# The last two gate blocks of a decoder layer, computed by halves of the tokens

## The chip, the cores and the metric

The kernel runs on one core of a Trainium2 chip. The metric is the time of the whole program on the device, in microseconds. The time before is 2029.54 us, the median of three runs (2029.25 to 2031.34).

## The reference

One decoder layer over 256 positions with 2048 features, in float32: a half-step SwiGLU, a mixer of a gated linear recurrence and a short convolution, a second half-step SwiGLU, then the part that the change touches:

```
gate = sigmoid(rms_norm(h, norm_ple) @ w_ple_gate)      # 2048 x 2048
h = h + gate * (p @ w_ple)                              # p has 256 features
return rms_norm(h, norm_final)

def rms_norm(x, g):
    r = rsqrt(mean(x * x, axis=-1) + EPS)               # over the features
    return x * r * g
```

The last norm needs the squares of all 2048 features of a token before it can scale any of them. Tokens are independent of each other in this stage.

## The kernel before, in words

Everything is kept transposed: `hT` is 128 partitions x 16 feature blocks x 256 tokens. A weight matrix is cut into blocks of 128 output features; a block is one *step* of a list. For a step, SP loads the block's weights (16 tiles of 128x128, 1 MB), two calls (L97 on ACT, L98 on DVE) split them into a high and a low part of type fp32r, and PE multiplies. The moving operand `xs[:, k, :]` holds for each of the 16 feature tiles the high part of 256 tokens and then their low part, 512 columns. `product` (L116) issues two matmuls per tile: the high weights with all 512 columns, and the low weights with the 256 high columns; both add up in one PSUM tile of 128x512, whose halves are added at the end (L146, L147). `product_one` (L124) issues three matmuls of 256 columns into the same 256 columns of PSUM, so that nothing is left to be added after the last one; it is used for the last block of a stage, where the next stage waits.

The stage at the end is `ple` (L787). Its 16 steps are the 16 blocks of `w_ple_gate`. The epilogue of a block (L824) multiplies by the row scale `rb` of the norm before (L153) and takes the sigmoid (L828). One step later `gated` (L850) multiplies by the block of p @ w_ple, adds to `hT`, adds the square to the running sum `acc` (L182, L183), and writes `hg`, the new h times the gain of the last norm (L855). The products p @ w_ple (L814) are spread over the earlier steps.

Block 15, the last, has an epilogue of its own: gate, sum and square by halves of the tokens in turn (L832 to L841), and a matmul with the squares as weights and one column of ones (L196) sums over the features, giving one number per token, on the token's partition; the running sum `acc` is added in the same way before it. After the loop over the steps (L958 to L969) the mean and the reciprocal root are made on 128x2 numbers (L201, then ten DVE instructions in `rsqrt`, L169), the result is put on the diagonal of two 128x128 tiles (L963), and a matmul with ones (L965, plain fp32, which PE executes as two passes) spreads it over all partitions. DVE multiplies `hg` by it in six pieces of 1, 2, 3, 3, 3 and 4 blocks (L968), and SP writes each piece out (L969).

The order of the work: the program is written step by step, and a planner orders the instructions of each engine by the time at which it expects their inputs. Between equally ready instructions the one written first goes first. On the chip each engine takes its queue in order and waits on semaphores. PSUM has eight buffers of 128x512 in rotation, the high and low parts of weights four of half a block each, small temporaries six.

Of the kernel before, what the change touches and what calls it, by code (L numbers as in the profile page):

```python
# [7 lines left out]
F32 = mybir.dt.float32  # L8
F32R = mybir.dt.float32r
I32 = mybir.dt.int32  # L10
AF = mybir.ActivationFunctionType
ALU = mybir.AluOpType
PSUM = bass.MemoryType.PSUM

P = 128
T = 256
T2 = 2 * T
NB = 16
NF = 44
NH = 8  # L20
EPS = 1e-6
# [6 lines left out]
C_FFN1, C_MIX, C_FFN2, C_PLE, C_FIN = 0, 16, 32, 48, 64  # L28
# [23 lines left out]
def kernel(  # L52
# [3 lines left out]
    nc = tc.nc  # L56
    V, A, TE = nc.vector, nc.scalar, nc.tensor
# [7 lines left out]
    hT = const.tile([P, NB, T], F32, name="hT")  # L65
    xs = const.tile([P, NB, T2], F32R, name="xs")
    cst = const.tile([P, NCST], F32, name="cst")
    ones = const.tile([P, P], F32, name="ones")
    ones_r = const.tile([P, P], F32R, name="ones_r")
    sel = const.tile([P, 2 * P], F32R, name="sel")  # L70
    acc = const.tile([P, T], F32, name="acc")
    rb = const.tile([P, T], F32, name="rb")
    rt = const.tile([P, 2], F32, name="rt")
# [3 lines left out]
    ident = cst[:, C_ID:C_ID + P]  # L77

    def tt(shape=(P, T), dtype=F32, tag="t", bufs=6):
        return tmp.tile(list(shape), dtype, tag=tag, name=tag, bufs=bufs)  # L80
# [49 lines left out]
    def weights(s, k):  # L130
        hi, lo = s.parts[k // s.half]
        return hi[:, k % s.half, :], lo[:, k % s.half, :]

    def products(s, ps, rhs, start=True, stop=True, ks=None, one=False):
        ks = range(s.nk) if ks is None else ks
        f = product_one if one else product
        for i, k in enumerate(ks):
            f(*weights(s, k), rhs(k), ps, start and i == 0, stop and i == len(ks) - 1)

    def new_ps():  # L140
        return psum.tile([P, T2], F32, tag="ps", name="ps")


    def halves(ps):
        t = tt()
        A.activation(t, ps[:, T:], AF.Copy)  # L146
        V.tensor_tensor(t, ps[:, :T], t, ALU.add)  # L147
        return t

    def scaled(ps, dst=None):  # L150
        t = halves(ps)
        dst = t if dst is None else dst
        V.tensor_tensor(dst, t, rb, ALU.mult)  # L153
        return dst
# [6 lines left out]
    def two(dst, src):  # L161
        A.activation(dst[:, :T], src, AF.Copy)  # L162
        V.tensor_tensor(dst[:, T:], src, dst[:, :T].bitcast(F32), ALU.subtract)
# [5 lines left out]
    def rsqrt(dst, v):  # L169
        V.tensor_scalar(dst.bitcast(I32), v.bitcast(I32), -0.5, MAGIC, ALU.mult, ALU.add)  # L170
        for _ in range(3):
            t = tt(shape=dst.shape)
            V.scalar_tensor_tensor(t, v, -0.5, dst, ALU.mult, ALU.mult)
            V.tensor_tensor(t, t, dst, ALU.mult)
            V.scalar_tensor_tensor(dst, t, 1.5, dst, ALU.add, ALU.mult)
# [19 lines left out]
    def token_sum(ps, src, i, first, last):  # L195
        TE.matmul(ps[i][:, 0:1], src[:, i * P:(i + 1) * P], ones[:, 0:1], start=first, stop=last)  # L196

    def token_scale(ps):
        v = tt(shape=(P, 2), tag="v2", bufs=1)
        for i in range(2):  # L200
            V.tensor_scalar(v[:, i:i + 1], ps[i][:, 0:1], 1.0 / (NB * P), EPS, ALU.mult, ALU.add)  # L201
        rsqrt(rt, v)
# [18 lines left out]
    steps = []  # L221

    def at(i, f):
        steps[i].hooks.append(f)

    def add(*a, **k):
        steps.append(Step(*a, **k))
        return len(steps) - 1

    st = {}  # L230

    def gemm_in(epi, one=False):
        def mm(s):
            s.ps = new_ps()
            products(s, s.ps, lambda k: xs[:, k, :], one=one)
        return mm, (lambda s: epi(s.ps))
# [549 lines left out]
    def ple():  # L786
        i0 = len(steps)  # L787
        m = st["ple"] = {}

        def open_ple(s):  # L790
            st["pool"] = ExitStack()
            p1 = m["pool"] = st["pool"].enter_context(tc.tile_pool(name="ple1", bufs=1))
            m["p"] = p1.tile([P, 2, T], F32, name="p")
            m["px"] = p1.tile([P, 2, T2], F32R, name="px")
            m["w"] = p1.tile([P, NB, 2 * P], F32, name="wpe")
            m["pe"] = p1.tile([P, NB, T], F32, name="pe")
            m["hg"] = p1.tile([P, NB, T], F32, name="hg")
            nc.sync.dma_start(m["p"], pT)
            for j in (0, 8):
                nc.sync.dma_start(m["w"][:, j:j + 8, :], w_pe[:, j:j + 8, :])  # L800

        def p_parts():
            for k in range(2):
                two(m["px"][:, k, :], m["p"][:, k, :])

        def pe_parts(j):
            hi = m["pool"].tile([P, 2, 2 * P], F32R, tag="pwh", name="pwh", bufs=2)
            lo = m["pool"].tile([P, 2, 2 * P], F32R, tag="pwl", name="pwl", bufs=2)
            w = m["w"][:, j:j + 2, :]
            A.activation(hi, w, AF.Copy)  # L810
            V.tensor_tensor(lo, w, hi.bitcast(F32), ALU.subtract)
            st["pw", j] = hi, lo

        def pe_mm(j):  # L814
            hi, lo = st["pw", j - j % 2]
            ps = new_ps()
            for k in range(2):
                sl = slice(k * P, (k + 1) * P)
                product(hi[:, j % 2, sl], lo[:, j % 2, sl], m["px"][:, k, :], ps, k == 0, k == 1)
            t = tt()  # L820
            A.activation(t, ps[:, T:], AF.Copy)
            V.tensor_tensor(m["pe"][:, j, :], ps[:, :T], t, ALU.add)

        def gate_epi(j):  # L824
            def epi(ps):
                s = st["s", j] = m["pool"].tile([P, T], F32, tag="sg", name="sg", bufs=4)
                if j < NB - 1:
                    A.activation(s, scaled(ps), AF.Sigmoid)  # L828
                    return
                token_sums_first()  # L830
                z, sq, h, pe = tt(), tt(), hT[:, j, :], m["pe"][:, j, :]
                for i in range(2):  # L832
                    a = slice(i * P, (i + 1) * P)
                    V.tensor_tensor(z[:, a], ps[:, a], rb[:, a], ALU.mult)
                    A.activation(s[:, a], z[:, a], AF.Sigmoid)
                for i in range(2):
                    a = slice(i * P, (i + 1) * P)
                    V.tensor_tensor(s[:, a], s[:, a], pe[:, a], ALU.mult)
                    V.tensor_tensor(h[:, a], h[:, a], s[:, a], ALU.add)
                    A.activation(sq[:, a], h[:, a], AF.Square)  # L840
                    token_sum(st["ts"], sq, i, False, True)  # L841
                A.activation(m["hg"][:, j, :], h, AF.Copy, scale=cst[:, C_FIN + j:C_FIN + j + 1])
            return epi

        def token_sums_first():
            st["ts"] = new_ps(), new_ps()
            for i in range(2):
                token_sum(st["ts"], acc, i, True, False)

        def gated(j):  # L850
            s, h = st["s", j], hT[:, j, :]
            V.tensor_tensor(s, s, m["pe"][:, j, :], ALU.mult)
            V.tensor_tensor(h, h, s, ALU.add)
            square_sum(j)
            A.activation(m["hg"][:, j, :], h, AF.Copy, scale=cst[:, C_FIN + j:C_FIN + j + 1])  # L855

        for j in range(NB):
            add(w_pg[j], NB, *gemm_in(gate_epi(j), one=j == NB - 1))
        at(i0, p_parts)
        for j in range(0, NB, 2):  # L860
            at(i0 + 1 + j // 2, lambda j=j: pe_parts(j))
            for d in range(2):
                at(i0 + 2 + j // 2, lambda j=j + d: pe_mm(j))
        for j in range(NB - 1):
            at(i0 + max(j, 2 + j // 2), lambda j=j: gated(j))
        steps[i0].before = open_ple
        return i0
# [30 lines left out]
    with tc.manual_schedule():  # L898
        for a, b in pieces:
            s = steps[a // 8]  # L900
# [10 lines left out]
        for j in range(NB):  # L911
            sq = sums[j] if j < 2 else tt()
# [41 lines left out]
        if s.after:  # L954
            s.after(s)


    m = st["ple"]  # L958
    ps = st["ts"]
    token_scale(ps)  # L960
    dg = tt()
    for i in range(2):
        V.tensor_scalar(dg[:, i * P:(i + 1) * P], ident, rt[:, i:i + 1], None, ALU.mult)  # L963
    ps = new_ps()
    TE.matmul(ps[:, :T], ones, dg, start=True, stop=True)  # L965
    for a, b in ((0, 1), (1, 3), (3, 6), (6, 9), (9, 12), (12, 16)):
        o = m["hg"][:, a:b, :]
        V.tensor_tensor(o, o, ps[:, :T].unsqueeze(1).broadcast_to([P, b - a, T]), ALU.mult)  # L968
        nc.sync.dma_start(out[:, a:b, :], o)  # L969
    st["pool"].close()  # L970


# [68 lines left out]
```

## Time and profile before

| | us |
|---|---|
| median of three runs | 2029.54 |
| the profiled execution | 2028.77 |
| its span | 2027.0 |
| PE busy in the span | 2002.1 |
| DVE busy | 1636.0 |
| ACT busy | 1117.1 |

The profile is of one execution. Its time is the span and 1.77 us around it. PE is the matmuls, PEld the loads of weights into PE, DVE and ACT the vector and scalar engines, SP the engine that issues the DMAs. A row such as `L196 PE MATMUL ps<-ones,acc 128*128 128x1 f32 x4` gives the line, engine and operation, the output and inputs by name, the shape, and how many instructions the row stands for. Matmuls are pipelined, so their listed durations overlap; the distance from start to start is what one costs. PEclk is the granted clock of PE as a share of 2.4 GHz.

### The profile page before, as it was taken

What the parts mean: (1) busy time and instruction counts of PE and PEld (TensorE: products, weight loads), DVE (VectorE), ACT (ScalarE), POOL (GpSimd) and SP (SyncE); (2) the same over time, 40 slices, a digit from 0 to 9 for tenths busy, and PEclk for the clock granted to TensorE, in tenths of its full rate; (3) what the DMA queues carried; (4) which work ended last, traced back from release to release, by engine and by line L of the source; (5) the groups of instructions that cost most, each with busy time, mean ns of one, the idle gap of its engine ahead of it and who ended that gap; (6) DMA issues with size and microseconds to landing.
All of it is one profiled execution on the core that took longest, in us unless ns stands there. A gap on an engine that the chain in (4) does not pass through costs nothing.

```text
span 2027.0 us, 28859 instructions
## 1 busy us (share of the span) xinstructions
PE 2002.1 (99%) x11094; PEld 1731.7 (85%) x11094; DVE 1636.0 (81%) x2645; ACT 1117.1 (55%) x1716; POOL 11.6 (1%) x23
## 2 busy tenths in 40 slices
PE   8999999999999999999999999999999999999997
PEld 7888888888888888888888888888888888888886
DVE  8988886888688775689798789788968886887886
ACT  7655555555555554553566556455555555555663
POOL 0000000000000000000000000000000000000000
PEclk9999999999999999999999999999999999999998
DMA  8686666665665465544355567766666666654742
GB/s 293 211 277 242 233 205 216 219 237 200 222 232 198 156 212 187 189 166 146 129 184 187 187 227 274 226 232 226 208 208 224 232 202 220 228 202 153 249 164 84
DMA packets 69546, 419.93 MB, mean 207 GB/s; under 512 B 7712, under 2 KB 7968, under 8 KB 35744
## 3 DMA queue, kind: packets, MB, share of 16 engines
q1 hardware_dynamic: 67104, 407.60, 59.0%
q0 software_dynamic: 2304, 10.49, 1.3%
q8 instruction: 87, 1.43, 0.3%
q14 instruction: 51, 0.42, 0.1%
HBM read 405.48 MB, written 12.58 MB: 206 GB/s over the span
## 4 chain that ended last, share of the span: by engine, by line
PE 89%; DVE 4%; DMA 4%; issue 1%; ACT 1%; SPq 0%; DVEq 0%; ACTq 0%
PE ps L120 49%; PE ps L119 23%; PE ps L294 3%; PE ps L295 3%; PE ps L293 3%; PE ps L122 2%; DVE lo L98 2%; DMA sraw<-w1s 1%; DMA raw<-w1d 1%; DMA raw<-w1u 1%; PE ps L591 1%; PE ps L494 1%; PE ps L493 1%; PE ps L492 1%; DMA sraw<-w2s 1%
## 5 line engine op out<-in xcount | busy, mean ns | idle before, releaser
L120 PE MATMUL ps<-xs,hi 128*128 128x512 f32 x3056 | 1082.8, 395 | 9.5 <-DVE xs L167 6.1
L98 DVE TENSOR_TENSOR lo<-raw,hi 128x1024 fp32r<-128x1024 f32 (+2 forms) x660 | 751.1, 1139 | 239.3 <-ACT hi L97 235.7
L97 ACT ACTIVATE hi<-raw 128x1024 fp32r<-128x1024 f32 (+2 forms) x660 | 652.7, 990 | 516.6 <-PE ps L120 323.6
L119 PE MATMUL ps<-xs,lo 128*128 128x256 f32 x2865 | 801.5, 280 | 0.4 <-DVE lo L98 0.2
L120 PEld LDWEIGHTS ps<-xs,hi 128*128 128x128 f32 x3056 | 569.7, 188 | 137.5 <-ACT hi L97 7.2
L119 PEld LDWEIGHTS ps<-xs,lo 128*128 128x128 f32 x2865 | 538.0, 188 | 10.4 <-DVE lo L98 1.8
L120 PE MATMUL ps<-hid,hi 128*128 128x512 f32 x1384 | 477.6, 394 | 0.0
L119 PE MATMUL ps<-hid,lo 128*128 128x256 f32 x1258 | 354.4, 283 | 0.5 <-ACT hid L162 0.5
L120 PEld LDWEIGHTS ps<-hid,hi 128*128 128x128 f32 x1384 | 251.5, 188 | 48.8
L119 PEld LDWEIGHTS ps<-hid,lo 128*128 128x128 f32 x1258 | 236.2, 188 | 7.3 <-ACT hid L162 1.3
L309 ACT ACTIVATE ahi<-sraw 128x1024 fp32r<-128x1024 f32 x48 | 51.0, 1063 | 125.2 <-DMA sraw<-w1s 61.5
L146 ACT ACTIVATE t<-ps 128x256 f32<-128x256 f32 x191 | 70.2, 372 | 88.3 <-PE ps L120 88.3
L320 DVE TENSOR_TENSOR st<-sraw 128x1024 f32<-128x1024 f32 x48 | 58.8, 1224 | 69.2 <-DMA sraw<-w1s 38.7
L147 DVE TENSOR_TENSOR t<-ps,t 128x256 f32<-128x256 f32 x191 | 80.3, 421 | 24.0 <-ACT t L146 23.9
L120 PE MATMUL ps<-mixout,hi 128*128 128x512 f32 x240 | 83.6, 397 | 0.0
L153 DVE TENSOR_TENSOR t<-t,rb 128x256 f32<-128x256 f32 x183 | 76.9, 422 | 2.7
L293 PE MATMUL ps<-bhi,xf 128*128 128x512 f32 x192 | 74.9, 390 | 0.0
L295 PE MATMUL ps<-blo,xf 128*128 128x512 f32 x192 | 74.9, 390 | 0.0
L294 PE MATMUL ps<-bhi,xf 128*128 128x512 f32 x192 | 74.9, 390 | 0.0
L208 DVE SCALAR_TENSOR_TENSOR hT<-ps,t 128x256 f32<-128x256 f32 x141 | 59.7, 424 | 13.7 <-DVE t L207 1.4
L207 DVE TENSOR_TENSOR t<-hT,t 128x256 f32<-128x256 f32 x141 | 59.1, 420 | 10.6 <-ACT t L206 10.6
L206 ACT ACTIVATE t<-ps 128x256 f32<-128x256 f32 x141 | 51.9, 369 | 27.5 <-PE ps L120 27.5
(234 smaller groups left out, 2078.7 us busy)
## 6 DMA issues: line engine op xcount, KB each, us to landing
raw<-w_in SPq DMA_DIRECT2D x48, 1024.0 KB, 4.8
raw<-w1d SPq DMA_DIRECT2D x48, 768.0 KB, 4.2
raw<-w2d SPq DMA_DIRECT2D x48, 768.0 KB, 4.3
raw<-w2g SPq DMA_DIRECT2D x32, 1024.0 KB, 4.9
raw<-w2u SPq DMA_DIRECT2D x32, 1024.0 KB, 5.1
raw<-w1u SPq DMA_DIRECT2D x31, 1024.0 KB, 5.3
raw<-w1g SPq DMA_DIRECT2D x30, 1024.0 KB, 5.0
xf<-forms SPq DMA_DIRECT2D x48, 640.0 KB, 4.0
```

The source lines that it names most:

```text
L97: A.activation(hi[:, sl, :], r, AF.Copy)
L98: V.tensor_tensor(lo[:, sl, :], r, hi[:, sl, :].bitcast(F32), ALU.subtract)
L119: TE.matmul(ps[:, T:], lo, m[:, :T], start=False, stop=False)
L120: TE.matmul(ps, hi, m, start=first, stop=last)
L146: A.activation(t, ps[:, T:], AF.Copy)
L147: V.tensor_tensor(t, ps[:, :T], t, ALU.add)
L153: V.tensor_tensor(dst, t, rb, ALU.mult)
L207: V.tensor_tensor(t, hT[:, j, :], t, ALU.add)
L208: V.scalar_tensor_tensor(hT[:, j, :], ps[:, :T], c, t, ALU.mult, ALU.add)
L293: TE.matmul(g[p], x_lo, hi[:, i, :], start=kp == 0, stop=False)
L294: TE.matmul(g[p], x_hi, hi[:, i, :], start=False, stop=False)
L295: TE.matmul(g[p], x_hi, lo[:, i, :], start=False, stop=kp == NK2 - 1)
```

## The change

The steps of the stage become 14 whole blocks, then blocks 14 and 15 for tokens 0 to 127, then blocks 14 and 15 for tokens 128 to 255. The second pair of steps loads and splits nothing; it takes the parts that the first pair made. A half step (`half_mm`) has the same number of matmuls as a whole one, each with half the columns: for block 14 one of 128 and one of 256 columns per feature tile (the first block of 256 has the high and low columns of the 128 tokens), for block 15 three of 128. Each half of block 15 is followed by its own token sums and its own last norm (`last_norm`): a reciprocal root on 128x1, one diagonal, one matmul of 128 columns, four products of 2, 4, 5 and 5 blocks with 128 tokens, and four DMAs. The part after the loop is gone. `hg` and the output are laid out by halves of the tokens; the host puts them back in order.

```diff
-            m["hg"] = p1.tile([P, NB, T], F32, name="hg")
+            m["hg"] = p1.tile([P, 2, NB, P], F32, name="hg")
...
+        def to_hg(j):
+            A.activation(m["hg"][:, :, j, :], hT[:, j, :].rearrange("p (w t) -> p w t", w=2), AF.Copy,
+                         scale=cst[:, C_FIN + j:C_FIN + j + 1])
...
+        def half_mm(j, w, last):
+            a = slice(w * P, (w + 1) * P)
+
+            def mm(s):
+                s.ps = new_ps()
+                for k in range(NB):
+                    hi, lo = weights(s, k)
+                    x = xs[:, k, :].rearrange("p (i t) -> p i t", i=2)[:, :, a]
+                    first, end = k == 0, k == NB - 1
+                    if last:
+                        TE.matmul(s.ps[:, :P], lo, x[:, 0], start=first, stop=False)
+                        TE.matmul(s.ps[:, :P], hi, x[:, 1], start=False, stop=False)
+                        TE.matmul(s.ps[:, :P], hi, x[:, 0], start=False, stop=end)
+                        continue
+                    ps = s.ps[:, :T].rearrange("p (i t) -> p i t", i=2)
+                    if not first:
+                        TE.matmul(ps[:, 1], lo, x[:, 0], start=False, stop=False)
+                    TE.matmul(ps, hi, x, start=first, stop=end)
+                    if first:
+                        TE.matmul(ps[:, 1], lo, x[:, 0], start=False, stop=False)
+            return mm
+
+        def half_epi(j, w, last):
+            a = slice(w * P, (w + 1) * P)
+
+            def epi(s):
+                h = hT[:, j, a]
+                t, u = tt(shape=(P, P)), tt(shape=(P, P))
+                if last:
+                    st["ts"] = st.get("ts", []) + [new_ps()]
+                    TE.matmul(st["ts"][w][:, 0:1], acc[:, a], ones[:, 0:1], start=True, stop=False)
+                    V.tensor_tensor(t, s.ps[:, :P], rb[:, a], ALU.mult)
+                else:
+                    A.activation(u, s.ps[:, P:T], AF.Copy)
+                    V.tensor_tensor(t, s.ps[:, :P], u, ALU.add)
+                    V.tensor_tensor(t, t, rb[:, a], ALU.mult)
+                A.activation(u, t, AF.Sigmoid)
+                V.tensor_tensor(u, u, m["pe"][:, j, a], ALU.mult)
+                V.tensor_tensor(h, h, u, ALU.add)
+                A.activation(t, h, AF.Square)
+                if last:
+                    TE.matmul(st["ts"][w][:, 0:1], t, ones[:, 0:1], start=False, stop=True)
+                else:
+                    V.tensor_tensor(acc[:, a], acc[:, a], t, ALU.add)
+                A.activation(m["hg"][:, w, j, :], h, AF.Copy, scale=cst[:, C_FIN + j:C_FIN + j + 1])
+                if last:
+                    last_norm(w)
+            return epi
+
+        def last_norm(w):
+            r, v = rt[:, w:w + 1], tt(shape=(P, 1), tag="v1", bufs=2)
+            V.tensor_scalar(v, st["ts"][w][:, 0:1], 1.0 / (NB * P), EPS, ALU.mult, ALU.add)
+            rsqrt(r, v)
+            dg = tt(shape=(P, P))
+            V.tensor_scalar(dg, ident, r, None, ALU.mult)
+            ps = new_ps()
+            TE.matmul(ps[:, :P], ones, dg, start=True, stop=True)
+            for a, b in ((0, 2), (2, 6), (6, 11), (11, 16)):
+                o = m["hg"][:, w, a:b, :]
+                V.tensor_tensor(o, o, ps[:, :P].unsqueeze(1).broadcast_to([P, b - a, P]), ALU.mult)
+                nc.sync.dma_start(out[:, w, a:b, :], o)
+
+        for j in range(NB - 2):
+            add(w_pg[j], NB, *gemm_in(gate_epi(j)))
+        two_last = []
+        for w in range(2):
+            for j in (NB - 2, NB - 1):
+                i = add(w_pg[j] if w == 0 else None, NB, half_mm(j, w, j == NB - 1), half_epi(j, w, j == NB - 1))
+                two_last.append(steps[i])
+                if w:
+                    def sp(s, of=two_last[j - NB + 2]):
+                        s.half, s.parts = of.half, of.parts
+                    steps[i].sp = sp
```

## Rows read from the trace of the kernel before

**Rows 1.** The page: busy time, share of the span and instructions of each engine.

```profile
PE 2002.1 (99%) x11094; PEld 1731.7 (85%) x11094; DVE 1636.0 (81%) x2645; ACT 1117.1 (55%) x1716; POOL 11.6 (1%) x23
```

**Rows 2.** Windows of blocks 14 and 15: length, busy us per engine, PEclk, DMA share, GB/s.

```profile
1999.84:2005.44 5.60, 5.60 (x34) 4.88 (x33) 3.69 (x8) 2.89 (x7) 0.00 (x0) 1.00 0.01 3
2005.44:2011.20 5.76, 5.76 (x50) 5.76 (x49) 2.55 (x6) 1.89 (x5) 0.00 (x0) 1.00 0.00 0
```

**Rows 3.** Chain that ended last, after the last matmul: start us, us, what.

```profile
2011.23 0.14 PE ps L128
...
2012.06 0.49 DVE sg L838 x2
...
2013.21 0.95 PE ps L196 x4
...
2014.18 0.17 DVE v L201
...
2016.34 0.49 DVE t L963 x2
...
2016.97 1.21 PE ps L965 x2
```

**Rows 4.** Timeline of DVE, final product: start, us, instruction, idle time and releaser.

```profile
2018.20 4.75 DVE L968 TENSOR_TENSOR hg<-hg,ps 128x256 f32<-128x256 f32 x6 [1.38 <-PE ps L965]
```

**Rows 5.** Timeline of SP, the issue of the last output DMA.

```profile
2022.97 0.33 SPq L969 DMA_DIRECT2D out_dram<-hg  x1
```

**Rows 6.** Timeline of PE: matmuls with 128, 512 and 256 columns.

```profile
972.31 1.95 PE L616 MATMUL ps<-Q,K 128*128 128x128 f32 x16
974.01 0.48 PE L120 MATMUL ps<-xs,hi 128*128 128x512 f32 x1
...
2005.20 0.39 PE L120 MATMUL ps<-xs,hi 128*128 128x512 f32 x1
2005.43 0.28 PE L126 MATMUL ps<-xs,lo 128*128 128x256 f32 x1
2005.55 0.28 PE L127 MATMUL ps<-xs,hi 128*128 128x256 f32 x1
```

**Rows 7.** Timeline of PE's weight loads: the four before matmuls of one column.

```profile
2011.07 0.54 PEld L196 LDWEIGHTS ps<-ones,acc 128*128 128x128 f32 x4
```

**Rows 8.** Line 196: weight loads, ns min/median/max, first and last start.

```profile
L196 PEld LDWEIGHTS ps<-ones,acc x16: 187/192/193, 43.1 to 2011.4; 128*128 128x128 f32 x16
...
L196 PEld LDWEIGHTS ps<-ones,t x4: 206/323/333, 2013.2 to 2013.7; 128*128 128x128 f32 x4
```

**Rows 9.** Timeline of PE's weight loads: a statistics matmul's load in the mixer.

```profile
1003.86 0.19 PEld L641 LDWEIGHTS ps<-sq,sel 128*128 128x128 f32 x1 [0.16 <-DVE sq L163]
```

**Rows 10.** Windows after the last matmul: columns as in rows 2.

```profile
2011.40:2013.30 1.90, 0.38 (x4) 0.30 (x3) 1.38 (x6) 0.96 (x5) 0.00 (x0) 1.00 0.00 0
2013.40:2018.20 4.80, 1.94 (x6) 1.16 (x6) 2.42 (x14) 0.36 (x1) 0.00 (x0) 0.50 0.00 0
```

**Rows 11.** Groups by form, final product: count, busy us, mean ns, idle before.

```profile
L968 DVE TENSOR_TENSOR hg<-hg,ps 128x1024 f32<-128x1024 f32 x1 | 1.2, 1216 | 0.0
...
L968 DVE TENSOR_TENSOR hg<-hg,ps 128x512 f32<-128x512 f32 x1 | 0.7, 681 | 0.0
```

**Rows 12.** DMA issues of the output: count, KB, median us to landing.

```profile
out_dram<-hg SPq DMA_DIRECT2D x1, 512.0 KB, 2.8
...
out_dram<-hg SPq DMA_DIRECT2D x1, 256.0 KB, 2.0
```

**Rows 13.** Window of the output's transfer: columns as in rows 2.

```profile
2019.60:2025.20 5.60, 0.00 (x0) 0.00 (x0) 3.35 (x4) 0.00 (x0) 0.00 (x0) 0.50 0.95 369
```

**Rows 14.** Timeline of PE around that statistics matmul.

```profile
1003.51 0.39 PE L120 MATMUL ps<-xs,hi 128*128 128x512 f32 x1
1003.74 0.28 PE L119 MATMUL ps<-xs,lo 128*128 128x256 f32 x1
1003.86 0.38 PE L641 MATMUL ps<-sq,sel 128*128 128x256 f32 x1
1004.08 0.39 PE L120 MATMUL ps<-xs,hi 128*128 128x512 f32 x1
```

More of the change, by code (lines that the diff above doesn't have):

```diff
@@ L826, in epi @@
                 s = st["s", j] = m["pool"].tile([P, T], F32, tag="sg", name="sg", bufs=4)
[L827 to L842, printed above, removed]
-            return epi
[L845 to L848, printed above, removed]
+                A.activation(s, scaled(ps), AF.Sigmoid)
+            return epi
         def gated(j):
@@ L854, in gated @@
             square_sum(j)
-            A.activation(m["hg"][:, j, :], h, AF.Copy, scale=cst[:, C_FIN + j:C_FIN + j + 1])
-        for j in range(NB):
-            add(w_pg[j], NB, *gemm_in(gate_epi(j), one=j == NB - 1))
+            to_hg(j)
+        def half_mm(j, w, last):
[18 more added lines that the diff above has]
+            return mm
@@ L863, in ple @@
                 at(i0 + 2 + j // 2, lambda j=j + d: pe_mm(j))
-        for j in range(NB - 1):
+        for j in range(NB - 2):
             at(i0 + max(j, 2 + j // 2), lambda j=j: gated(j))
@@ L955 @@
             s.after(s)
[L958 to L969, printed above, removed]
     st["pool"].close()
@@ L1034 @@
             for k, v in arrays.items()]
-    args.append(nc.dram_tensor("out_0_dram", (P, NB, T), F32, kind="ExternalOutput").ap())
+    args.append(nc.dram_tensor("out_0_dram", (P, 2, NB, P), F32, kind="ExternalOutput").ap())
     with tile.TileContext(nc) as tc:
@@ L1039 @@
     got = r.results[0]["out_0_dram"]
-    return np.ascontiguousarray(got.transpose(1, 0, 2).reshape(NB * P, T).T).reshape(1, T, NB * P)
+    return np.ascontiguousarray(got.transpose(1, 3, 2, 0)).reshape(1, T, NB * P)
```

## The prediction

> **What bounds the kernel now.** Read the share of each engine first: PE is busy for 99% of the span [rows 1], so elsewhere almost everything lies beside matmuls. The change is confined to the end, so the next view is the busy time by window there. Block 14 of the gate takes 5.60 us and block 15 takes 5.76 us, with PE busy throughout at a granted clock of 1.00 [rows 2]. PE is the bound up to the last matmul of block 15, at 2011.37. Then comes the chain of waits [rows 3]: from 2011.37 nothing is hidden any more. DVE and ACT make the gate, PE sums the squares over the features, ten small DVE steps make the reciprocal root, PE spreads it over the partitions, and at 2018.20 DVE starts on the final product. That is 6.83 us after the last matmul. The final product takes DVE 4.75 us for six pieces [rows 4]; the last piece is issued at 2022.97 [rows 5], and the span ends at 2027.0, 4.03 us later. The exposed tail is 15.63 us: 6.83 + 4.77 to the last issue + 4.03.
>
> The change trades that: the first 128 tokens go through this tail beneath the matmuls of the second 128, and the price is that two blocks run as four half blocks. The question is what a half block costs on PE, and what is left exposed.
>
> **The matmuls.** Before, the two blocks are 32 + 48 = 80 pairs of a weight load and a matmul. After, every weight tile is loaded once for each half of the tokens: 2 x 32 + 2 x 48 = 160 pairs. The moving columns in sum stay the same; only their number per load halves. So the term is the time of a pair with 128 columns. A pair with 512 columns takes 0.23 us and one with 256 takes 0.12 [rows 6]; block 14 has 0.350 us for one of each [rows 2], so 0.233 and 0.117. If columns alone set the pace, 128 would take 0.059. The trace has pairs with fewer columns, though. Sixteen with 128 columns take 974.01 - 972.31 = 1.70 us, 0.106 each [rows 6], and these are plain fp32, which may stream more slowly. Four with one single column settle it better: their loads spread over 0.54 us [rows 7], of which the last takes 0.19 [rows 8], so 0.35 / 3 = 0.117 apart, and next to nothing was streamed. A load of 128 columns costs about as much as 256 moving columns, and 256 columns is just where the two meet. I take 0.112 for the pair with 128 columns, between 0.106 and 0.117; both ends stay in the range.
>
> [...]
>
> After: block 14, twice 16 pairs with 128 (lo) and 16 with 256 (hi) columns, 32 x (0.112 + 0.117) = 7.33 us. Block 15, twice 48 pairs, 96 x 0.112 = 10.75. Six short fp32 pairs now stand between the halves (running sum of squares, squares of block 15, spreading of the scale, two each), 6 x 0.112 = 0.67; before, they all came after the last matmul. Together 18.75 against 5.60 + 5.76 = 11.36: the last matmul ends 7.4 us later (6.6 with 0.106, 8.1 with 0.117).
>
> No load or split of weights is added: the second half reads the parts made for the first, in four buffers that no later block wants. DMA moves nothing in this stretch (share 0.01 and 0.00 [rows 2]), and DVE is busy 3.69 and 2.55 us of these windows, so the small epilogues of the first halves and the first half's 2.5 us of final product find room.
>
> **The tail of the second half.** From the last matmul to the final product the same chain runs on 128 tokens, not two times 128 in turn. The gate part saves the doubled step, 0.1 us. The token sum: before, four pairs in 0.95 us, then the scale step [rows 3]; with two pairs the step starts about 0.45 earlier. The ten steps after it, on 128x1 in place of 128x2, cost as before: from 2014.18 to 2016.34, some 0.2 us each with their gaps [rows 3]. One diagonal in place of two: 0.49 becomes 0.29, 0.2 saved. Spreading the scale: 1.21 us [rows 3] at a granted clock of 0.50, that is 1.2 GHz; PE stopped at 2011.4, had 1.00 until about 2013.3 and 0.50 after it [rows 10]. Half the columns save 0.4 at 1.2 GHz, 0.8 if the clock is still at 2.4 GHz. Together 1.1 to 1.5; I take 1.35. The gap becomes 5.5 us.
>
> The final product: a piece of 512 elements takes 0.68 us, one of 1024 1.22 [rows 11], so 1.04 ns an element plus some 0.15, most of which overlaps between pieces. Half the elements in four pieces of 256, 512, 640 and 640: about 2.48 us against 4.75, 2.27 saved. The last piece carries 320 KB in place of 512. Landing took 2.8 us for 512 KB and 2.0 for 256 [rows 12], so 2.2 to 2.3: 0.5 saved. The queue moved 369 GB/s over 5.60 us for all 2.1 MB [rows 13]; half of that needs 2.8 us and the second half's issues are spread over 2.5, so the transfer doesn't become the limit. The close of the program (2027.0 less 2022.97 and 2.8) stays. Saved in all: 1.35 + 2.27 + 0.5 = 4.1 us (3.8 to 4.4).
>
> **Sum.** 7.4 - 4.1 = +3.3 us. The rest of the kernel is untouched (one activation per block has another view of the same elements, on ACT with 2.7 us idle in 5.6). The profiled execution took 2028.77 us, 1.77 around a span of 2027.0; it becomes 2032.1. That run is 0.77 below the median of 2029.54, so the median to expect is 2032.8. With the bounds of the terms (6.6 - 4.4 to 8.1 - 3.8) it is 2031.7 to 2033.8.
>
> **The added waits.** The first half's squares and scale come back to PE through ACT and DVE some 1.7 and 4.9 us after its last matmul, and PE takes its queue in order: were they queued where the program writes them, the matmuls of the second half would stand behind them. But the planner places instructions by when it thinks them ready: one statistics matmul (L641), written ahead of the next block, stands among that block's matmuls [rows 14], and its load waited only 0.16 us for DVE [rows 9]. So I cost these two waits at 0.2 to 0.3 in all, within the range. If the planner thinks the half blocks shorter than they are, the first half's product comes late instead, and the second half's first DVE step waits behind at most its 2.5 us.
>
> **Rivals.**
> (1) Columns set the pace, not loads: 32 x (0.059 + 0.117) + 96 x 0.059 + 0.67 = 11.96 us, 0.6 more than before, less 4.1: -3.5 us, 2026.0. For it: column time fits 512 and 256 well. Against: the one-column pairs. [...] 12%.
> (2) The planner queues the first half's norm too early and PE waits for it. Place: the token sum and the spreading, ahead of the second half of block 14 or 15. All of it costs up to 5.5 - 0.45 = 5 us, 2037.8, and as PE then stands still the clock may fall to 1.2 GHz, where a load took 0.32 us in place of 0.19 [rows 8]. It decides from 0.8 us of waiting: then slower by more than 0.2%. Against it: the matmul that the planner let the next block's pass [rows 9, 14]. 15%.
> (3) The clock falls in the half blocks. The trace has no 5 us of such short matmuls, so nothing shows that it holds. One half of block 15 at 1.2 GHz costs 48 x 0.1 = 4.8 us more: 2037.6. 6%.
>
> **Chances.** The forecast has 65%, with 2031.2 to 2034.4 as its own range; the three rivals as above, 2% for the rest. A difference of 0.2%, 4.06 us, is about what a measurement of this kernel can tell from none. The forecast, +3.3, lies just inside: I put a quarter of its 65% above 2033.6. With (2) and (3) that gives 38% slower; faster is a quarter of (1) and a little, 4%; 58% within. The range of 2029.0 to 2037.0 leaves out (1) and the ends of (2) and (3).
>
> **What would show it.** In the changed kernel's trace: half of block 14 takes 3.66 us and of block 15 5.4 us, weight loads 0.11 us apart; PE without gaps between the halves; the first half's output issued before the last matmul; last matmul to final product 5.5 us, final product 2.5, last issue to end 3.5. The prediction is wrong if pairs with 128 columns start 0.06 us apart, or if PE shows waits of over 0.8 us on ACT or DVE in the second half.

## The result, and the profile after

The changed kernel takes 2041.88 us (median of six runs, 2039.46 to 2047.58), the kernel before 2029.39 in runs beside it (six, 2026.99 to 2031.34). The ratio is 1.0068, with a 95% interval of 1.0057 to 1.0078: slower, by 12.5 us between the medians. The forecast was 2032.8 with a range up to 2037.0, so the time lies outside it. The profiled execution took 2045.22 us, with a span of 2043.4.

First the busy shares of the changed kernel, to be read against [rows 1]: 82 more matmuls, of which 80 are the doubled pairs of the half blocks and two the second spreading.

```profile
PE 2015.4 (99%) x11176; PEld 1741.1 (85%) x11176; DVE 1637.6 (80%) x2662; ACT 1117.0 (55%) x1721; POOL 11.6 (1%) x23
```

In these two profiles block 14 starts 5.1 us apart (1999.84 and 2004.96), although ahead of it the code differs only in the view through which `hg` is written. In all the profiles of this study it starts somewhere from 1999.8 to 2006.7: the chain of waits holds DMAs for 5% of the span, some 100 us, nearly all ahead of it, and these waits scatter. So what the change does is read from one stretch, from the first matmul of block 14 to the end of the span. It takes 27.16 us before (1999.84 to 2027.0) and 38.48 after (2004.96 to 2043.44), 11.3 more. The changed kernel, run once more unchanged, has 38.65. The kernel before, run once more, agrees from the first matmul of block 15 to the end: 21.21 against 21.56 us. So the stretch repeats within 0.4 us where whole times scatter by 2 us or more to either side.

The windows of the changed kernel's stretch, with the columns of [rows 2] and, for the last line, [rows 10]:

```profile
2004.96:2008.62 3.66, 3.66 (x33) 3.66 (x32) 2.80 (x6) 2.03 (x4) 0.00 (x0) 1.00 0.02 4
2008.62:2013.93 5.31, 5.31 (x50) 5.31 (x49) 2.78 (x9) 2.31 (x7) 0.00 (x0) 1.00 0.00 0
2014.10:2015.70 1.60, 0.16 (x2) 0.07 (x1) 0.88 (x3) 0.50 (x2) 0.00 (x0) 1.00 0.00 0
2015.80:2019.40 3.60, 0.94 (x4) 0.88 (x4) 2.03 (x12) 0.31 (x2) 0.00 (x0) 0.50 0.00 0
2019.47:2025.90 6.43, 6.43 (x32) 6.43 (x32) 2.48 (x4) 0.00 (x0) 0.00 (x0) 0.50 0.44 163
2026.24:2031.50 5.26, 5.26 (x49) 5.26 (x49) 1.46 (x5) 1.19 (x4) 0.00 (x0) 1.00 0.01 3
2031.70:2037.40 5.70, 1.49 (x7) 1.08 (x5) 2.91 (x15) 0.91 (x3) 0.00 (x0) 0.60 0.00 0
```

Lines 1 and 2 are the first half of the tokens, blocks 14 and 15: as forecast, at full clock. Lines 3 and 4 are what wasn't forecast: between the halves PE is busy 0.16 and 0.94 us of 5.2. In line 4 the granted clock has fallen to 0.50, 1.2 GHz; PE's last block matmul started at 2013.82, the two short ones behind it had ended by 2014.26, and the drop shows at 2015.74. Line 5 is the second half of block 14, which took 3.66 us in line 1 and now takes 6.77 (to 2026.24), all but the end of it at 1.2 GHz though PE is busy throughout; the clock is back at 2025.98. Line 6, the second half of block 15, has its 5.3 us again.

The timeline of PE (start, us, instruction, and in brackets its idle time and who ended it) shows who holds PE up between the halves:

```profile
2013.70 0.27 PE L854 MATMUL ps<-xs,hi 128*128 128x128 f32 x1
2013.82 0.28 PE L855 MATMUL ps<-xs,hi 128*128 128x128 f32 x1
2013.93 0.33 PE L873 MATMUL ps<-ones,acc 128*128 128x1 f32 x2
2015.87 0.59 PE L884 MATMUL ps<-ones,t 128*128 128x1 f32 x2 [1.61 <-ACT t L882]
2019.05 0.77 PE L899 MATMUL ps<-t,ones 128*128 128x128 f32 x2 [2.60 <-DVE t L897]
2019.47 0.56 PE L860 MATMUL ps<-xs,hi 128*128 128x256 f32 x1
```

The planner has put the three matmuls of the first half's norm where the program writes them, ahead of the second half's first matmul (L860), and PE takes its queue in order. L884 waits 1.61 us for the squares, L899 2.60 us for the diagonal that the reciprocal root gives. Of the 5.54 us from 2013.93 to 2019.47, the six short pairs were forecast with 0.67.

Last, the tail of the changed kernel, from DVE's, SP's and the DMAs' views, against [rows 4, 5, 12]:

```profile
2037.47 2.48 DVE L902 TENSOR_TENSOR hg<-hg,ps 128x256 f32<-128x256 f32 x4 [0.95 <-PE ps L899]
...
2039.98 0.33 SPq L903 DMA_DIRECT2D out_dram<-hg  x1
...
out_dram<-hg SPq DMA_DIRECT2D x2, 320.0 KB, 2.3
```

The last matmul ends at 2031.72. The gap up to the final product is 5.75 us (6.83 before), the product 2.48 (4.75), the last issue to the end 3.46 (4.03). The tail is 11.7 us against 15.6.

So the 11.3 us are: +7.25 for the matmuls of the halves (2 x 3.66 + 2 x 5.31 + 0.67, less 11.36), -3.9 for the tail, +4.87 for the time between the halves (5.54 less 0.67), in which PE mostly stood, +3.11 for 1.2 GHz in the second half of block 14 (6.77 less 3.66).

### The profile page after: what moved, and what is told of

Read it like the earlier page. It is cut to its first block, busy times and chain, and to the rows that moved or that the text cites. A ratio compares the mean times of both kernels' runs of the same rounds, so it can differ in the third digit from the quotient of the medians.

```text
span 2043.4 us, 29055 instructions
## 1 busy us (share of the span) xinstructions
PE 2015.4 (99%) x11176; PEld 1741.1 (85%) x11176; DVE 1637.6 (80%) x2662; ACT 1117.0 (55%) x1721; POOL 11.6 (1%) x23
## 4 chain that ended last, share of the span: by engine, by line
PE 86%; DVE 5%; DMA 5%; issue 1%; ACT 1%; SPq 0%; DVEq 0%; ACTq 0%
PE ps L120 48%; PE ps L119 22%; PE ps L293 3%; PE ps L294 3%; PE ps L295 3%; DMA sraw<-w2s 2%; PE ps L122 2%; DMA sraw<-w1s 2%; DVE lo L98 2%; DVE blo L310 1%; PE ps L591 1%; PE ps L494 1%; PE ps L493 1%; PE ps L492 1%; ACT ahi L309 1%
```

## The experiments

The theory after the result: the waits and the clock cost 8 us, and the rest is the forecast. What had to be told apart was whether the waits cause the clock's fall, whether the half blocks cost what they do because of their loads, and why the planner ordered these matmuls so when in [rows 14] it let the next block's matmuls pass one of the kind.

**1. The first half's norm placed later.** The token sum stands after nine feature tiles of the second half's block 14, the spreading after five tiles of block 15.

```diff
+                    if w and k == (5 if last else 9):
+                        st["late"].pop(0)()
...
-                    TE.matmul(st["ts"][w][:, 0:1], t, ones[:, 0:1], start=False, stop=True)
+                    def sums():
+                        TE.matmul(st["ts"][w][:, 0:1], t, ones[:, 0:1], start=False, stop=True)
...
-                    last_norm(w)
+                    todo = st["late"] = [lambda: (sums(), last_root(w)), lambda: last_norm(w)]
+                    while w and todo:
+                        todo.pop(0)()
```

> The first half's token sum is written after nine feature tiles of the second half of block 14, its spreading after five tiles of the second half of block 15, so PE's queue comes to them later than their inputs. Theory (PE stood still in its queue, and the clock fell because of it): the waits of 1.61 and 2.60 us and the 1.2 GHz stretch are gone, half blocks of 3.66 and 5.3 us, from the first matmul of block 14 to the end of the span 38.4 - 8.0 = 30.4 us against 27.2 before, so +3.3 us, ratio to before 1.0016 (1.0010 to 1.0025). Rival (the short matmuls themselves lose the clock, or the first half's product on DVE holds up the second half): the stretch stays above 34 us and the ratio above 1.003.

Measured: 2035.68 us (eight runs) beside 2030.33 (fourteen), ratio 1.0027 (1.0016 to 1.0037). The stretch is 30.37 us, 3.2 more than before: the forecast's sum, +3.3. By the whole time it is 5.4 us, a ratio just above the 1.0025 that was expected at most. PE's timeline and two windows of this kernel, columns as above:

```profile
2012.00 0.33 PE L862 MATMUL ps<-xs,hi 128*128 128x256 f32 x1
2012.17 0.28 PE L887 MATMUL ps<-ones,t 128*128 128x1 f32 x2
2012.31 0.31 PE L861 MATMUL ps<-xs,lo 128*128 128x128 f32 x1
...
2015.62 0.44 PE L908 MATMUL ps<-t,ones 128*128 128x128 f32 x2
2015.81 0.31 PE L855 MATMUL ps<-xs,lo 128*128 128x128 f32 x1
```

```profile
2010.02:2014.00 3.98, 3.98 (x37) 3.98 (x36) 2.14 (x11) 0.91 (x3) 0.00 (x0) 1.00 0.00 0
2014.06:2019.50 5.44, 5.44 (x51) 5.44 (x51) 4.39 (x13) 1.19 (x4) 0.00 (x0) 1.00 0.17 57
```

Neither statistics matmul waits, PE is busy in all of both windows, and the clock stays at 1.00. In the stretch, waits and clock are the whole miss, and the other terms hold.

**2. Token sums and spreading in block 15's own PSUM tile**, so that the norm asks for no tile of its own.

```diff
-                    st["ts"] = st.get("ts", []) + [new_ps()]
+                    st["ts"] = st.get("ts", []) + [s.ps[:, T:]]
...
-            ps = new_ps()
+            ps = st["ts"][w][:, P:]
```

> Written order as in the change, but token sums and spread scale go to unused columns of block 15's own PSUM tile, so that the norm takes no new tile from the rotation. Theory (the planner kept the order because the second half's tile came behind the norm's tiles in the rotation): PE's queue now has the token sum after 8 matmuls of the second half and the spreading after 16 more. The chip's chains are 1.8 and 3.2 us long, so PE still waits some 0.7 and 1.2 us, and the clock holds: +3.3 + 1.9 = about +5.2 us, ratio 1.0026 (1.0015 to 1.0040). Rival (the rotation had nothing to do with it): order and waits as in the changed kernel, +11 to +12.5 us, ratio 1.0057 or more.

Measured: 2039.78 us (six runs) beside 2030.33, ratio 1.0046 (1.0032 to 1.0059). The planner's order changes as expected: the token sum goes after 10 pairs of the second half's block 14, the spreading after 13 more, and PE's waits shrink to 0.53 and 0.97 us. But the planner still expects the norm's steps sooner than they come, and the time expected, a ratio of 1.0040 at most, was missed. PE's timeline and two windows of the profiled run:

```profile
2015.30 0.38 PE L884 MATMUL ps<-ones,t 128*128 128x1 f32 x2 [0.53 <-ACT t L882]
...
2018.19 0.80 PE L899 MATMUL ps<-t,ones 128*128 128x128 f32 x2 [0.97 <-DVE t L897]
```

```profile
2013.38:2017.60 4.22, 3.32 (x27) 2.97 (x26) 2.44 (x13) 0.91 (x3) 0.00 (x0) 1.00 0.00 0
2018.70:2030.70 12.00, 12.00 (x59) 12.00 (x57) 3.85 (x9) 1.19 (x4) 0.00 (x0) 0.50 0.24 89
```

The clock fell at 2017.77, in the second wait, and 12 us of matmuls without a gap did not bring it back, so this run's stretch is 38.84 us. That isn't so in every run: in two of the six the mean granted clock was 0.994 (2043.37 and 2044.84 us), in the other four 0.997 to 0.998 (2036.84 to 2041.32). The order follows the tile; whether waits of 0.5 and 1 us cost the clock differs, by these means, from run to run.

**3. PE kept busy in the waits**, by 14 and 22 unused matmuls of 256 columns ahead of the two that wait.

```diff
+                    if w == 0:
+                        fill(s, 14)
...
+        def fill(s, n):
+            ps = new_ps()
+            for i in range(n):
+                TE.matmul(ps[:, :T], weights(s, i % NB)[0], xs[:, i % NB, :T], start=True, stop=True)
...
+            if w == 0:
+                fill(s, 22)
```

> Order as in the change; ahead of the two waiting matmuls of the first half, 14 and 22 matmuls of 256 columns whose results nothing uses, 1.64 and 2.57 us of PE work in place of standing still. Theory (of the 11.3 us, some 4.9 are waiting and 3.1 to 3.7 the clock): the granted clock stays at 2.4 GHz through the second half, its block 14 takes 3.66 us in place of 6.77, spreading about 0.4 in place of 0.77; +7.5 to +8.2 us to before, ratio 1.0037 to 1.0041. Rival (the second half of block 14 is slow for another reason, such as DMA of the first half's output or DVE): it stays near 6.8 us, and the ratio at 1.0057 or more.

Measured: 2040.51 us (five runs) beside 2030.33, ratio 1.0046 (1.0034 to 1.0058). The stretch is 35.03 us, +7.87, inside what was expected; by the whole time it is 10.2, above the 8.2 expected at most. PE's timeline, then windows of the filled wait and of the second half of block 14:

```profile
2013.24 0.33 PE L873 MATMUL ps<-ones,acc 128*128 128x1 f32 x2
...
2018.39 0.36 PE L860 MATMUL ps<-xs,hi 128*128 128x256 f32 x1
```

```profile
2013.43:2018.36 4.93, 4.93 (x42) 4.85 (x41) 2.92 (x15) 0.92 (x3) 0.00 (x0) 1.00 0.00 0
2018.39:2022.10 3.71, 3.71 (x34) 3.71 (x34) 2.48 (x4) 0.00 (x0) 0.00 (x0) 1.00 0.53 186
```

The waits for the squares and the diagonal are still there, but PE works in them, the clock keeps 1.00, and the second half of block 14 has 3.7 us, not 6.8. So the 3.1 us are the clock's, and the clock fell because PE stood; it wasn't the half blocks. Between the halves there are 5.15 us here and 5.54 in the change: 0.4 of the 4.87 us booked there are the clock's too, for the short matmuls at 1.2 GHz. By the stretches, 38.48 against 35.03, the clock cost 3.45 us in all.

**4. No norm between the halves**: blocks by halves, both norms after the last matmul with one reciprocal root for both.

```diff
+                if last and w:
+                    for f in st["sums"]:
+                        f()
+                    token_scale(st["ts"])
+                    last_norm(0)
+                    last_norm(1)
```

> Half blocks as in the change, but token sums, root and spreading of both halves come after the last matmul, the root for both halves at once; nothing of the first half's norm is hidden beneath the second half. Theory: PE has only the price of the halves, 2 x 3.66 + 2 x 5.31 = 17.9 us against 11.36, +6.6; the tail is that of before with a shorter chain and a smaller last piece, -1.0 to -1.5: +5 to +5.6 us, ratio 1.0025 to 1.0028, and no clock loss within the blocks. Rival (hiding the first half is worth nothing): no slower than the kernel with the late norm, ratio at most 1.0016.

Measured: 2037.19 us (five runs) beside 2030.33, ratio 1.0032 (1.002 to 1.0044); stretch 32.85, +5.69, just above the 5.6 expected at most (6.9 by the whole time). The final product is as long as before:

```profile
2028.59 4.88 DVE L906 TENSOR_TENSOR hg<-hg,ps 128x256 f32<-128x256 f32 x8 [0.75 <-PE ps L903]
```

Against experiment 1, 2.5 us of the stretch: that is what running the first half's norm beneath the second half is worth, once it waits for nothing. The halving itself costs more than that.

**5. Fewer loads in block 15**: as experiment 1, with two loads a tile (256 and 128 columns) in place of three (128). Block 15's epilogue gains an eviction and an addition by it, and the spreading stands after eight of its tiles, not five.

```diff
-                    if last:
+                    if False:
                         TE.matmul(s.ps[:, :P], lo, x[:, 0], start=first, stop=False)
```

> The late norm, and block 15 in halves in the form of block 14: per feature tile 256 + 128 columns with two weight loads in place of 3 x 128 with three. The same columns, fewer loads. Theory (loads set the pace of short matmuls): half a block 15 takes 3.66 us in place of 5.3, the first matmul of block 14 to the end 30.4 - 3.3 + 0.6 (an eviction and an addition more in the exposed chain) = 27.7 us against 27.2 before: ratio 1.0000 to 1.0010. Rival (the columns or the count of tiles set the pace): half a block 15 stays near 5.3 us and the stretch near 30.4.

Measured: 2036.64 us (seven runs) beside 2031.73 (seventeen), ratio 1.0029 (1.0017 to 1.0041). A half of block 15 takes 3.66 us in place of 5.30, with the same columns: the loads set the pace. But the stretch is 30.52 us, not 27.7. The first halves of both blocks in one window, waits of PE (us in total, times, longest) and two lines of DVE's timeline:

```profile
2004.34:2011.60 7.26, 7.26 (x65) 7.26 (x63) 4.73 (x12) 3.74 (x9) 0.00 (x0) 1.00 0.01 2
```

```profile
PE ps L885 <- ACT t L882: 3.4, 1, 3.4
...
PE ps L875 <- DVE acc L887: 1.2, 1, 1.2
```

```profile
2020.70 2.14 DVE L909 TENSOR_TENSOR hg<-hg,ps 128x512 f32<-128x512 f32 x3
2022.76 0.28 DVE L877 TENSOR_TENSOR t<-ps,t 128x128 f32<-128x128 f32 x1
```

With the shorter block the running sum of block 14 is not ready when PE wants it (L875, 1.2 us), and the last block's gate (L877) stands behind the first half's product (L909) on DVE, for which PE then waits 3.4 us where it waited 1.6 in the change. The 3.3 us of loads came back almost whole as two waits; the second is the one that the prediction named for a product that comes late.

**6. The norm and output by halves alone**, the two blocks whole as before.

```diff
-        for j in range(NB - 2):
+        for j in range(NB - 1):
             add(w_pg[j], NB, *gemm_in(gate_epi(j)))
...
+        def last_epi(ps):
+            for w in range(2):
+                half_epi(NB - 1, w, ps)
+            token_scale(st["ts"])
+            for w in range(2):
+                last_norm(w)
+        add(w_pg[NB - 1], NB, *gemm_in(last_epi, one=True))
```

> Blocks 14 and 15 whole as before, the last norm by halves after the last matmul, output by halves: the tail's part of the change alone, with nothing hidden. Theory: no price on PE, the tail of the kernel with both norms after (1.0 us shorter than before, from a shorter first spreading and a smaller last piece): 26.2 us from the first matmul of block 14 to the end against 27.2 before, ratio 0.9990 to 1.0000, not told apart in the whole time. Rival (smaller pieces of output cost the DMA more than they save): 27.2 or more.

Measured: 2031.42 us (eleven runs) beside 2031.73, ratio 0.9999 (0.999 to 1.0008). From block 15's first matmul to the end it takes 21.17 us, the kernel before 21.56 and 21.21 in its two profiles. From block 14's first matmul it is 26.77 us, against 27.16 and 26.81. The gain expected, 1.0 us, isn't there. So the layout by halves costs nothing, and without the halved blocks it gives nothing.

**7. Still fewer columns**: as experiment 1, but 14 of the 16 feature tiles of block 15's halves multiply 64 of their 128 tokens. It leaves out the products of the other tokens.

```diff
+                        c = P if first or end else P // 2
+                        TE.matmul(s.ps[:, :c], lo, x[:, 0, :c], start=first, stop=False)
...
```

> The late norm; in block 15's halves 14 of the 16 feature tiles are multiplied with 64 of the 128 tokens only (the other tokens' sums lack them). Three loads per tile as before, half the columns. Theory (a pair of load and matmul takes 0.11 us whatever it streams below 256 columns): half a block 15 stays at 5.3 us, the stretch at 30.4. Rival (columns count, plus a fixed part): some 0.03 us less per pair, 42 pairs a half, 4.0 us a half and a stretch near 28.

Measured, one run: 2049.01 us, stretch 40.48, where 30.4 was expected and 28 by the rival. PE's timeline where the pace changes, and windows before it, after it and near the end:

```profile
2013.94 0.28 PE L856 MATMUL ps<-xs,lo 128*128 128x64 f32 x1
2014.05 0.28 PE L857 MATMUL ps<-xs,hi 128*128 128x64 f32 x1
2014.17 0.28 PE L858 MATMUL ps<-xs,hi 128*128 128x64 f32 x1
2014.28 0.38 PE L856 MATMUL ps<-xs,lo 128*128 128x64 f32 x1
2014.47 0.40 PE L857 MATMUL ps<-xs,hi 128*128 128x64 f32 x1
2014.68 0.40 PE L858 MATMUL ps<-xs,hi 128*128 128x64 f32 x1
```

```profile
2011.00:2014.00 3.00, 3.00 (x29) 3.00 (x28) 1.81 (x6) 1.29 (x4) 0.00 (x0) 1.00 0.00 0
2014.50:2016.50 2.00, 2.00 (x11) 2.00 (x11) 0.32 (x2) 0.60 (x2) 0.00 (x0) 0.50 0.00 0
2028.50:2034.50 6.00, 6.00 (x30) 6.00 (x30) 2.48 (x4) 0.00 (x0) 0.00 (x0) 0.50 0.49 177
```

Pairs with 64 columns start 0.11 us apart, like those with 128: the load is the whole price. But from 2014.3 on the pairs are 0.21 apart: the clock has fallen amid matmuls in unbroken succession, and it stays at 0.50 to the end. With one run it isn't shown that the short columns did it; in experiment 1, with 128 columns and the same order, none of eight runs lost the clock.

**8 and 9. What the planner waits for.** In 8 the norm asks for its two PSUM tiles at the start of the half's block 14, ahead of block 15's tile, and first writes them where the change does. In 9 a matmul of one column also writes into the spreading's tile at once.

```diff
+                if not last:
+                    st["early"] = st.get("early", []) + [new_ps(), new_ps()]
+                    TE.matmul(st["early"][2 * w + 1][:, 0:1], ones, ones[:, 0:1], start=True, stop=True)
...
-                    st["ts"] = st.get("ts", []) + [new_ps()]
+                    st["ts"] = st.get("ts", []) + [st["early"][2 * w]]
...
-            ps = new_ps()
+            ps = st["early"][2 * w + 1]
```

(8 is this without the third added line.)

> As the change, but the two PSUM tiles of each half's norm are asked for ahead of block 15's tile, and first written where the change writes them. Theory (a tile is taken from the rotation in the order of asking, at its first write, so the second half's tile has to wait until the spreading has taken its own): PE's order and both waits stay as in the change, some 1.6 and 2.6 us, the stretch from the first matmul of block 14 to the end 38 to 39 us. Rival (the tile counts as taken when it is asked for): the second half's matmuls pass, waits under 1.3 us.

> As before, and one matmul of one column writes into the spreading's tile at once, ahead of block 15 (its result is overwritten). Theory (the rotation): now the second half's matmuls pass the norm: the token sum comes after some 10 pairs, the spreading after some 14 more, which is still earlier than the chip's chains of 1.8 and 3.2 us: waits of about 0.5 and 1.4 us, the stretch 27.2 + 3.3 + 1.9 + 0.2 = 32.6 us with the clock held, up to 39 if it falls as in the kernel with tiles in the same bank. Rival (only the shared bank freed the order there): waits as in the change, 1.6 and 2.6 us.

Measured for 8, one run: 2040.12 us, stretch 37.59, a little under the 38 to 39 expected, as the clock came back sooner after the waits; order and waits are the change's own, 1.61 and 2.60, on PE's timeline:

```profile
2009.64 0.33 PE L875 MATMUL ps<-ones,acc 128*128 128x1 f32 x2
2011.59 0.38 PE L886 MATMUL ps<-ones,t 128*128 128x1 f32 x2 [1.61 <-ACT t L884]
2014.57 0.77 PE L901 MATMUL ps<-t,ones 128*128 128x128 f32 x2 [2.60 <-DVE t L899]
2014.98 0.56 PE L862 MATMUL ps<-xs,hi 128*128 128x256 f32 x1
```

Measured for 9: 2038.7 us (seven runs) beside 2029.84 (ten), ratio 1.0046 (1.0032 to 1.0059); the stretch of the profiled run is 32.58, counted from the matmul of one column ahead of block 14, as expected; the whole time is 8.9 us above the kernel before. On its timeline the second half's matmuls pass the norm's:

```profile
2017.10 0.33 PE L863 MATMUL ps<-xs,hi 128*128 128x256 f32 x1
2017.56 0.38 PE L887 MATMUL ps<-ones,t 128*128 128x1 f32 x2
2017.81 0.31 PE L862 MATMUL ps<-xs,lo 128*128 128x128 f32 x1
...
2019.27 0.22 PE L862 MATMUL ps<-xs,lo 128*128 128x128 f32 x1
2020.45 0.49 PE L902 MATMUL ps<-t,ones 128*128 128x128 f32 x2 [0.96 <-DVE t L900]
2020.69 0.37 PE L863 MATMUL ps<-xs,hi 128*128 128x256 f32 x1
```

One write of one column, and the waits go from 1.61 and 2.60 us to 0.14, too short to be listed, and 0.96. Asking early changes nothing, the first write does: the planner hands out PSUM tiles in order of asking, when it places the first write into each; the orders of 2, 8 and 9 all fit this. The second half's tile is asked for after the spreading's, so its matmuls can't be placed until the spreading is, and the spreading can't until the planner expects its diagonal.

**10 and 11. Both kernels once more, unchanged**, one run each, for the scatter of the stretch.

> The kernel before, unchanged: a second profile, to see how well the stretch from the first matmul of block 14 to the end repeats. 27.2 us within 0.3.

> The changed kernel, unchanged: a second profile. Both waits within 0.1 us of 1.61 and 2.60; the stretch may differ from 38.5 by how long the clock stays down after the second wait: 35 us were it not to fall, 43 were it to stay down to the end.

Measured: 2031.57 and 2044.6 us. The kernel before has a stretch of 26.81 us, just under the 27.2 within 0.3 that was expected. The changed kernel's stands with the result; its waits on PE are 1.61 and 2.60 us again, and its clock falls (2015.43) and returns (2025.67) as in the first profile.

No run beats the kernel before by what can be measured; the best, 6, equals it.

## Why the prediction was wrong, point by point

**The step that failed is "The added waits".** It put PE's two waits at 0.2 to 0.3 us, because the planner had let the next block's matmuls pass a statistics matmul [rows 9, 14]. The time between the halves took 4.87 us more than the short matmuls were given, and the second half of block 14 took 3.11 more at 1.2 GHz: 8.0 us, of which experiment 3 shows 3.45 to be the clock's and the rest PE's waiting. When the inputs would come it had right: 1.7 and 4.9 us after the half's last matmul, and they were used 1.8 and 5.0 us after it; what failed was that PE would have other matmuls to do until then. Rival 2, with 15%, came in full: its bound for the waits was 5 us, and it said that the clock may fall, but its 2037.8 held nothing for that. The evidence was true and didn't bear on the case. What the profile shows of [rows 14] is an order of two matmuls, not what each needs a buffer for: in the code, L641 adds into a tile that L640, written just ahead of it, has begun, so it never waits to be given one. In the change the second half's tile comes after the norm's tiles in the rotation; that this is the cause, experiments 8 and 9 show between them. The code had it in plain sight: a `new_ps()` in `last_norm`, ahead of the `new_ps()` of the next step.

**The matmuls** were right: a half of block 14 was put at 3.66 us and took 3.66, a half of block 15 at 5.4 and took 5.31; the term came to 7.25 against 7.4. Rival 1, columns set the pace, is out: 128 and 64 columns take the same 0.11 us, and experiment 5 saves 1.64 us a half for 16 loads fewer. The Trainium skill (page "TensorE: Matmul & The Clock Gate", section "Weight-path perf modes — Fast Weight Load (FWL) and DoubleRow") has the fast weight load on when there are 128 weights and the input type is not FP32. For these fp32r weights none shows: their loads are listed with 0.19 us [rows 9], like those of fp32 weights [rows 8].

**The tail** was right: 3.9 us saved against 4.1. The gap was put at 5.5 and is 5.75: the spreading ran at 1.2 GHz again, for which the prediction's lower end of the saving, 1.1 us, would have given 5.7; product 2.48 and end 3.46 are as forecast.

**The sum** without waits, +3.3, is what experiment 1 shows by the stretch, +3.2, while the whole time has 5.4, with an interval of +0.16 to +0.37%, or 3.2 to 7.5 us. The forecast's 4.06 us for a difference that can be told lies within it; even with these waits gone the change doesn't pay.

**Rival 3**, the clock falls in the half blocks, didn't happen in the first halves of the change nor in experiment 1, all at 1.00. In the one run of experiment 7, with 64 columns, it did.

What stays open: whole times differ by 12.5 us where the stretch shows 11.3. One such difference would be within the scatter of the waits ahead of block 14. But in each of experiments 1, 3, 4, 5 and 9 too the medians lie further above the kernel before than the stretch does, by 1.2 to 3.4 us; in experiment 6, with whole blocks, they do not. So halving the blocks seems to cost some 2 us more than the stretch shows. Block 14 starts at 2004.1 on average in the ten profiles with half blocks and at 2001.9 in the three without, but no run singles out a cause. Why the clock came back in the second half of the change and not before the end in the profiles of experiments 2 and 7 was not settled either.

## What to carry to other kernels

Cutting the moving side of a matmul below the columns at which its weight load is hidden buys no time on PE: here 256 columns were that point, and halving them added 7.25 us to save 3.9 in the tail. Before work is slid beneath another block's matmuls, look at which buffers of a rotation it asks for ahead of that block, for these fix the order whatever the dependences allow. A forecast that has a wait of PE as a rival should give the clock's price with it: here 3.45 of 8 us.

## What the runs showed of the hardware that had not been expected

- The clock can fall without any wait of PE: in experiment 7's one run, 64-column pairs in unbroken succession at 1.00 up to 2014.3, then 0.21 us a pair in place of 0.11, at 0.50 for the 33 us to the end of the span, in the first 21 of which PE had no gap.
- Once at 1.2 GHz, PE did not get 2.4 GHz back in 12 us of unbroken short matmuls (experiment 2, profiled run); in the change it did, at 2025.98, after it had worked without a gap from 2019.47.
- The same kernel seems to keep or lose the clock from run to run: in experiments 2 and 9 three of thirteen runs had a mean granted clock of 0.994, and the other ten 0.997 or 0.998. In the changed kernel all six had 0.996 or less, in experiments 1 and 3 all thirteen at least 0.997.
